# The state space branch of a hybrid block with its features on partitions

## The chip, the cores and the metric

One Trainium2 chip, of which the kernel uses one core. The metric is the device time of one execution in microseconds; less is better. The profile gives the span of one execution, from its first instruction to its last, and all rows of the trace are of that execution.

## The reference

Two layers of a decoder trunk on 512 tokens of width 1024, batch 1, all in float32. Each layer normalises `x`, multiplies it by one combined input matrix, runs three branches on pieces of the result (a Mamba-2 state space branch, latent attention, a gated delta rule), merges their projections by gates, and ends with a feed-forward part. The change touches only the state space branch:

```python
def ssd_mixer(z, xbc, dt_raw, conv_w, conv_b, dt_bias, a_log, d_skip, norm_g):
    # G = 2 groups, E = 8 heads a group, P = 64 features a head, N = 128 states
    xbc = silu(causal_dwconv(xbc, conv_w) + conv_b)
    xs, bm, cm = split(xbc, ...)
    dt = softplus(dt_raw + dt_bias); a = -exp(a_log)
    y = ssd_chunked(xs * dt[..., None], dt * a, bm, cm)
    y = y + d_skip[:, :, None] * xs
    y = y.reshape(S, SSD_INNER) * silu(z)
    y = rmsnorm(y.reshape(S, G, SSD_INNER // G), norm_g)

def ssd_chunked(X, dA, Bm, Cm):              # chunks of 128 tokens, 4 of them
    A_cum = cumsum(A)                        # within a chunk
    L = exp(where(tril, A_cum[l] - A_cum[s], -inf))
    y_diag = einsum('bcgls,bgecls,bcsgep->bclgep', Cc @ Bc.T, L, X)
    states = einsum('bclgn,bgecl,bclgep->bcgepn', Bc, exp(A_cum[-1] - A_cum), X)
    # h_prev: states carried from chunk to chunk, times exp(A_cum[-1])
    y_off = einsum('bclgn,bcgepn,bgecl->bclgep', Cc, h_prev, exp(A_cum))
    return y_diag + y_off
```

## The kernel before

Tokens are 4 tiles of 128 (`T` = 4), features 8 tiles of 128 (`KD` = 8). The normalised input lies with features on partitions, as a pair `xh`, `xl` of a rounded part and its rest. Every dense product is three TensorE matmuls of 512 moving columns (`mm3`, L181 to L183): high by high, high by low, low by high. Weights come in pieces of 512 KB over SP's DMA queue (`weights_raw`, L160, two buffers); ScalarE casts each half to its rounded part (L153), VectorE forms the rest (L154), with four buffers of each. `dense_F` leaves the result with features on partitions (the weights are stationary), two PSUM banks at a time where its piece has 256 columns; `dense_T` leaves it with tokens on partitions (the activations are stationary), four banks, one for each tile of tokens. Both take the same number of matmuls for the same weights. The PSUM banks are four for dense products (`acc`), three for small ones (`sm`) and one apart (`yt`, from `y_bank`).

A plain float32 product (operands not split, as in all small products of the state space branch) shows as two records of TensorE for each instruction, two passes.

`step_sizes`, run once a layer during the attention, computes the step sizes, the running sums of the decays and their exponentials with tokens on partitions (`dtq`, `cum`, `dec`). It writes the running sums to DRAM (`d_c`) with heads on rows, from where `seg_exp` broadcasts four heads' rows to all partitions (L455) and forms the decay matrix exp(-relu(cum[s] - cum[l])) of each head on ScalarE (L457, L458), into the tile `eE`, which has the source token s on partitions.

`ssd_group(g)` handles 8 heads. It projects and convolves B and C (`bt`, `ctl`, features on partitions), turns B to tokens on partitions (L700), projects and convolves the 512 inputs in four tiles (`xf`), and turns each by four transposes on TensorE (L708) which ScalarE copies to `xs`, tokens on partitions (L709). The gate `z` is projected by `dense_T` through `silu_T`, tokens on partitions. Then come four chunks, each with

- C times B of the chunk, masked (`cb`, L721, L723), times the decay matrices (L725);
- the inputs times the step sizes (`xd`, L727) and eight products, one for each head, with the 128 x 128 decay matrix stationary and the head's 64 inputs moving (L730);
- the skip term and the sum (L732, L733);
- from the second chunk on, C of the chunk times the carried state in one product of 512 columns (L736), scaled by the decay (L738) and added (L739);
- in all but the last, the new state (L742 to L750);
- the gate (L752) and the sum of squares over the group's 512 features, which lie on the free axis, by ScalarE's accumulator (L754).

After the chunks the row scale is formed (`rsq`, L264 and L265), the tokens' rows are scaled by it (L758), four times four transposes bring features to partitions (L763, bank `yt`), and `split_gain` (L260, L261) applies the norm's gain, a scalar for each partition there, and splits into `yh`, `yl`, the input of the branch's output projection much later.

The order of the work: `ssd_group(0)`, `gdn_decays`, half of the attention's output projection, `ssd_group(1)`, the other half, the delta-rule branch. The instructions of each engine are put in one order ahead of time by a scheduler that goes by the order of the program, by priorities and by its own estimates, so dense products of the following projection run between the chunks' small ones. On the chip each engine takes its list in that order, and so does SP with the DMAs. The big tiles of all branches share a ring of four buffers named `tok`.

## Time and profile before

| what | value |
|---|---|
| device time, median of 3 runs | 2338.18 us (2336.49 to 2344.52) |
| the profiled execution: its span | 2334.6 us |
| what lies around the span, against the median of the runs | 3.6 us |
| mean granted TensorE clock | 0.996 |
| TensorE matmul busy | 2294.8 us, 98% of the span |
| TensorE weight load busy | 1891.3 us, 81% |
| VectorE busy | 1582.1 us, 68% |
| ScalarE busy | 1159.8 us, 50% |
| DMA moved | 240.38 MB, 103 GB/s on average |

How to read it: the profile lists no device time of the profiled execution apart from its span, so a difference is worked out on the span, and the median of the runs lies 3.6 us above that. Matmuls are pipelined and their ends are modelled: the time of one is read from the start of one record to the start of the next. An engine's idle time counts only where TensorE waits for it.

### The profile page before, as it was taken

How to read it: one execution, taken by the hardware profiler on the slowest of the kernel's cores; microseconds unless marked ns; L12 is line 12 of the kernel's file. 1: busy time of each engine (PE TensorE's matmuls, PEld its weight loads, DVE VectorE, ACT ScalarE, POOL GpSimd, SP SyncE). 2: the span in 40 equal slices, each digit the busy share in tenths (PEclk: the TensorE clock that was granted, in tenths of full speed). 3: DMA queues.
4: the chain of work that ended last, by engine and by line, in shares of the span. 5: the costliest groups of instructions: out<-in, count | busy, mean ns of one | idle time of the engine just before them, and what ended most of it. 6: DMA issues, size and time to landing. Idle time of an engine off the chain costs nothing.

```text
span 2334.6 us, 32156 instructions
## 1 busy us (share of the span) xinstructions
PE 2294.8 (98%) x11926; PEld 1891.3 (81%) x11926; DVE 1582.1 (68%) x3100; ACT 1159.8 (50%) x2403; POOL 58.6 (3%) x74
## 2 busy tenths in 40 slices
PE   8999999999999999999999999999999999999998
PEld 7788787878887888888888887888788878888886
DVE  6776656875675458668767765667756645677668
ACT  6656644333443345545656557443334434545545
POOL 0000000000000000000010000000000000000000
PEclk9999999999999999999999999999999999999999
DMA  4323533352222443243132235334422224333231
GB/s 136 87 63 92 169 101 109 109 154 73 86 69 72 140 150 108 73 127 108 44 101 81 82 91 170 101 105 139 118 82 86 68 77 158 126 118 100 91 109 46
DMA packets 208221, 240.38 MB, mean 103 GB/s; under 512 B 33920, under 2 KB 155456, under 8 KB 208064
## 3 DMA queue, kind: packets, MB, share of 16 engines
q1 hardware_dynamic: 204544, 233.07, 32.7%
q10 hardware_dynamic: 3520, 5.25, 0.9%
q8 instruction: 94, 1.54, 0.3%
q14 instruction: 63, 0.52, 0.1%
HBM read 221.41 MB, written 11.63 MB: 100 GB/s over the span
## 4 chain that ended last, share of the span: by engine, by line
PE 86%; DVE 7%; DMA 3%; ACT 2%; POOL 1%; issue 1%; ACTq 0%; SPq 0%; DVEq 0%; POOLq 0%
PE acc L181 22%; PE acc L182 22%; PE acc L183 22%; PE sm L183 2%; PE sm L182 2%; PE sm L181 2%; DVE wlo L154 1%; PE sm L730 1%; DMA eE<-d_c 1%; DVE tok L846 1%; DMA mix<-mix 1%; PE sm L633 1%; DVE gQ L845 1%; PE yt L182 1%; PE sm L1003 1%
## 5 line engine op out<-in xcount | busy, mean ns | idle before, releaser
L154 DVE TENSOR_TENSOR wlo<-wraw,whi 128x512 fp32r<-128x512 f32 x552 | 378.3, 689 | 429.2 <-ACT whi L153 412.4
L153 ACT CAST whi<-wraw 128x512 fp32r<-128x512 f32 x552 | 341.4, 621 | 598.0 <-PE acc L182 371.0
L183 PE MATMUL acc<-xh,wlo 128*128 128x512 f32 (+1 forms) x1184 | 460.9, 390 | 0.0
L181 PE MATMUL acc<-xh,whi 128*128 128x512 f32 (+1 forms) x1184 | 460.7, 390 | 0.0
L182 PE MATMUL acc<-xl,whi 128*128 128x512 f32 (+1 forms) x1184 | 460.0, 389 | 0.0
L183 PEld LDWEIGHTS acc<-xh,wlo 128*128 128x128 f32 x1184 | 223.6, 189 | 41.9
L182 PEld LDWEIGHTS acc<-xl,whi 128*128 128x128 f32 x1184 | 223.5, 189 | 42.0 <-DVE xl L261 0.4
L181 PEld LDWEIGHTS acc<-xh,whi 128*128 128x128 f32 x1184 | 223.2, 189 | 41.7 <-ACT xh L260 0.4
L181 PE MATMUL acc<-yh,whi 128*128 128x512 f32 x384 | 151.9, 399 | 0.0
L182 PE MATMUL acc<-yl,whi 128*128 128x512 f32 x384 | 151.4, 394 | 0.0
L183 PE MATMUL acc<-yh,wlo 128*128 128x512 f32 x384 | 151.3, 394 | 0.0
L183 PE MATMUL acc<-whi,xl 128*128 128x512 f32 (+1 forms) x384 | 144.0, 375 | 0.0
L182 PE MATMUL acc<-wlo,xh 128*128 128x512 f32 (+1 forms) x384 | 143.9, 375 | 0.0
L181 PE MATMUL acc<-whi,xh 128*128 128x512 f32 (+1 forms) x384 | 142.6, 374 | 0.0
L674 DVE SCALAR_TENSOR_TENSOR ckl<-acc,pc,ckl 128x511 f32<-128x511 f32 (+2 forms) x168 | 120.4, 744 | 16.9 <-ACT ckl L670 8.3
L153 ACT CAST whi<-wr 128x512 fp32r<-128x512 f32 x128 | 79.5, 621 | 68.2 <-PE acc L183 32.7
L183 PE MATMUL acc<-whi,yl 128*128 128x512 f32 x256 | 99.7, 389 | 0.0
L181 PE MATMUL acc<-whi,yh 128*128 128x512 f32 x256 | 99.7, 389 | 0.0
L182 PE MATMUL acc<-wlo,yh 128*128 128x512 f32 x256 | 99.6, 389 | 0.0
L154 DVE TENSOR_TENSOR wlo<-wr,whi 128x512 fp32r<-128x512 f32 x128 | 85.8, 686 | 12.5 <-ACT whi L153 11.7
L181 PEld LDWEIGHTS acc<-yh,whi 128*128 128x128 f32 x384 | 71.7, 188 | 16.8 <-ACT yh L260 1.7
L182 PEld LDWEIGHTS acc<-yl,whi 128*128 128x128 f32 x384 | 72.2, 188 | 15.3 <-issue 1.0
(411 smaller groups left out, 4545.3 us busy)
## 6 DMA issues: line engine op xcount, KB each, us to landing
wraw<-in_w_in_dram SPq DMA_DIRECT2D x148, 512.0 KB, 3.6
wraw<-in_w_up_dram SPq DMA_DIRECT2D x64, 512.0 KB, 3.6
wr<-in_w_down_dram SPq DMA_DIRECT2D x32, 1024.0 KB, 5.0
eE<-d_c SPq DMA_DIRECT2D x48, 256.0 KB, 4.0
wraw<-in_w_mla_out_dram SPq DMA_DIRECT2D x16, 512.0 KB, 3.4
eE<-d_e SPq DMA_DIRECT2D x32, 256.0 KB, 3.0
wraw<-in_w_ssd_out_dram SPq DMA_DIRECT2D x16, 512.0 KB, 3.4
wraw<-in_w_gdn_out_dram SPq DMA_DIRECT2D x16, 512.0 KB, 3.3
```

Of the source, the lines that this page charges most:

```text
L153: act.copy(hi, raw)
L154: dve.tensor_tensor(lo, raw, f32(hi), ALU.subtract)
L181: pe.matmul(o, ah, bh, start=start, stop=False, skip_group_check=more)
L182: pe.matmul(o, ah, bl, start=False, stop=False, skip_group_check=more)
L183: pe.matmul(o, al, bh, start=False, stop=stop, skip_group_check=more)
L633: pe.transpose(ps[:, n : n + P], pn[t][:, kb * P : (kb + 1) * P], ident)
L674: dve.scalar_tensor_tensor(acc[:, d:], ps[:, : S - d], taps_[3 - d], acc[:, d:], ALU.mult, ALU.add)
L730: pe.matmul(py[:, h * 64 : (h + 1) * 64], e2[h // 4][:, h % 4, :], xd[:, h * 64 : (h + 1) * 64], start=True, stop=True)
L845: dve.tensor_tensor(pd, bc_last(nb[:, m, m + 1 :], m + 1), bc_mid(xb[:, m, : m + 1], 31 - m), ALU.mult)
L846: dve.tensor_tensor(xb[:, m + 1 :, : m + 1], xb[:, m + 1 :, : m + 1], pd, ALU.add)
L1003: pe.matmul(po[:, h * P : (h + 1) * P], pt_[:, h, :], vn[:, h * P : (h + 1) * P], start=True, stop=True)
```

## The change

The branch keeps its features on partitions to the end. The four convolved input tiles stay in `xf`, which now has a big buffer of its own; the transposed inputs are multiplied by the step sizes on the way out of PSUM (`xd`), and `xf` is then scaled in place by the skip factor, a column of parameters now. The gate is projected by `dense_F`, in two pieces of two tiles. In a chunk a head's 64 inputs are stationary, its decay matrix moves, and the two heads of a feature tile write the lower and the upper 64 partitions of one bank. The product with the carried state has four stationary pieces of 128 state columns and C moving; its decay, which now varies along the free axis, comes as a broadcast from a second DRAM copy of the exponentials (`d_p`, written in `step_sizes`), two DMAs a chunk. The sum of squares runs over partitions: a square on ScalarE, two adds on VectorE over the four feature tiles, and a product with a column of ones into the `yt` bank. The row scale goes to DRAM (`d_r`) and comes back as a broadcast over partitions; a product on VectorE with gain and row scale and `split_act` (L256, L257) take the place of the scaling, the transposes and `split_gain`. The ring `tok` has five buffers in place of four.

```diff
--- before.py
+++ after.py
@@ -31,7 +31,7 @@
 HALVES = (slice(0, S // 2), slice(S // 2, S))
 PARAMS = ('gdn_conv_w', 'ssd_conv_w', 'ssd_conv_b', 'norm1_g', 'ssd_norm_g', 'mla_q_norm_g', 'mla_kv_norm_g',
           'gdn_norm_g', 'norm2_g')
-ROWS = ('ssd_dt_bias', 'gdn_dt_bias', 'ssd_a_log', 'gdn_a_log', 'ssd_d')
+ROWS = ('ssd_dt_bias', 'gdn_dt_bias', 'ssd_a_log', 'gdn_a_log')
 
 
 def shape_constants():
@@ -299,9 +299,9 @@
 
 
     def load_params(ly, rows=True):
-        pc = mk(sp, [P, 155], F32, "pc", 2)
+        pc = mk(sp, [P, 163], F32, "pc", 2)
         sync.dma_start(pc, a["pcols"][ly])
-        prow = mk(sp, [P, 64], F32, "prow", 2)
+        prow = mk(sp, [P, 48], F32, "prow", 2)
         if rows:
             load_rows(prow, ly)
         return pc, prow
@@ -357,7 +357,7 @@
         gconv = lambda j, c: pc[:, j * 16 + c : j * 16 + c + 1]
         sconv = lambda j, c: pc[:, 64 + j * 12 + c : 64 + j * 12 + c + 1]
         col = lambda i: pc[:, 112 + i : 113 + i]
-        sconv_b, g_n1, g_ssd, g_q, g_kv, g_gdn, g_n2 = 0, 12, 20, 28, 32, 34, 35
+        sconv_b, g_n1, g_ssd, g_q, g_kv, g_gdn, g_n2, c_d = 0, 12, 20, 28, 32, 34, 35, 43
 
 
         sw = small_weights(small_raw(ly)) if ly else small_weights(raws0[0], False)
@@ -394,7 +394,8 @@
         dve.tensor_copy(sv, ps.rearrange("p (t n) -> p t n", t=T)[:, :, 64:96])
 
         cum = mk(sp, [P, T, 24], F32, "cum")
-        d_c = mk(dr, [T, 24 * P], F32, "d_c", 2)
+        d_c, d_p = (mk(dr, [T, 24 * P], F32, n, 2) for n in ("d_c", "d_p"))
+        d_r = mk(dr, [2, S], F32, "d_r", 2)
 
         def step_sizes():
 
@@ -433,6 +434,9 @@
             rows = mk(ml, [96, P], F32, "crow")
             act.copy(rows, pc_[:96, :P])
             sync.dma_start(d_c.rearrange("t (n l) -> (t n) l", l=P), rows)
+            prows = mk(ml, [96, P], F32, "crowe")
+            act.activation(prows, pc_[:96, :P], AF.Exp)
+            sync.dma_start(d_p.rearrange("t (n l) -> (t n) l", l=P), prows)
             dec = mk(sp, [P, 3, T, 24], F32, "dec")
             act.activation(dec.rearrange("p i t n -> p (i t n)"), ps[:, :288], AF.Exp)
             ndec = mk(sp, [P, T, 8], F32, "ndec")
@@ -442,8 +446,8 @@
             dve.tensor_scalar(beta, beta, 0.5, 0.5, ALU.mult, ALU.add)
             dtq = mk(sp, [P, T, 16], F32, "dtq")
             dve.tensor_scalar(dtq, spl[:, :, 0:16], 0.25, None, ALU.mult)
-            dsk = mk(sp, [P, 16], F32, "dsk")
-            dve.tensor_scalar(dsk, prow[:, 48:64], 0.25, None, ALU.mult)
+            dsk = mk(sp, [P, 8], F32, "dsk")
+            dve.tensor_scalar(dsk, pc[:, 112 + c_d : 120 + c_d], 0.25, None, ALU.mult)
             tap("spl", spl)
             tap("dec", dec)
             tap("beta", beta)
@@ -684,8 +688,7 @@
 
         def ssd_group(g, yh, yl):
             h0 = 8 * g
-            xs = mk(br, [P, T, 512], F32, "tok", 4)
-            z = mk(br, [P, T, 512], F32, "tok", 4)
+            xf, xd, z = (mk(br, [P, T, 512], F32, "tok", 5) for _ in range(3))
             bt, ctl = (mk(br, [P, S], F32, "ft", 6) if g else mk(lp, [P, S], F32, f"ckh{i}") for i in range(2))
             btok = mk(br, [P, T, P], F32, "kt", 2)
 
@@ -701,16 +704,22 @@
             act.activation(btok.rearrange("p t n -> p (t n)"), ps, AF.Copy, scale=0.25)
             for cp in range(2):
                 for j, pj in enumerate(dense_F(weights(w_in, O_XBC + 512 * g + 256 * cp, 256, D), tiles(256), D, xh, xl)):
-                    xf = mk(br, [P, S], F32, "ft4", 2)
-                    conv(pj, 4 * g + 2 * cp + j, xf)
+                    c = 2 * cp + j
+                    conv(pj, 4 * g + c, xf[:, c, :])
                     ps = sm_bank()
                     for t in range(T):
-                        pe.transpose(ps[:, t * P : (t + 1) * P], xf[:, t * P : (t + 1) * P], ident)
-                    act.copy(xs[:, :, (2 * cp + j) * P : (2 * cp + j + 1) * P], ps.rearrange("p (t n) -> p t n", t=T))
-            silu_T(br, O_SZ + 512 * g, z)
+                        pe.transpose(ps[:, t * P : (t + 1) * P], xf[:, c, t * P : (t + 1) * P], ident)
+                    th = lambda x: x.rearrange("p t (h n) -> p t h n", h=2)
+                    dve.tensor_tensor(th(xd[:, :, c * P : (c + 1) * P]), th(ps.rearrange("p (t n) -> p t n", t=T)),
+                                      bc_last(dtq[:, :, h0 + 2 * c : h0 + 2 * c + 2], 64), ALU.mult)
+                    act.activation(xf[:, c, :], xf[:, c, :], AF.Copy, scale=dsk[:, 4 * g + c : 4 * g + c + 1])
+            for cp in range(2):
+                for j, pj in enumerate(dense_F(weights(w_in, O_SZ + 512 * g + 256 * cp, 256, D), tiles(256), D, xh, xl)):
+                    silu2(z[:, 2 * cp + j, :], pj)
 
             hv8 = lambda x: x.rearrange("p (h n) -> p h n", h=8)
-            ss = mk(sp, [P, T], F32, "sss")
+            c4 = lambda x: x.rearrange("p (c l) -> p c l", c=4)
+            pss = y_bank()
             st = None
             for t in range(T):
                 tok = slice(t * P, (t + 1) * P)
@@ -723,23 +732,25 @@
                 dve.scalar_tensor_tensor(cb, ps[:, :P], 0.25, incl, ALU.mult, ALU.mult)
                 for e in e2:
                     dve.tensor_tensor(e, e, bc_mid(cb, 4), ALU.mult)
-                xd = mk(br, [P, 512], F32, "wk0")
-                dve.tensor_tensor(hv8(xd), hv8(xs[:, t, :]), bc_last(dtq[:, t, h0 : h0 + 8], 64), ALU.mult)
                 py = sm_bank()
-                for h in range(8):
-                    pe.matmul(py[:, h * 64 : (h + 1) * 64], e2[h // 4][:, h % 4, :], xd[:, h * 64 : (h + 1) * 64], start=True, stop=True)
-                y = mk(br, [P, 512], F32, "wk1")
-                dve.tensor_tensor(hv8(y), hv8(xs[:, t, :]), bc_last(dsk[:, h0 : h0 + 8], 64), ALU.mult)
-                dve.tensor_tensor(y, y, py, ALU.add)
+                for c in range(4):
+                    for i in range(2):
+                        h = 2 * c + i
+                        pe.matmul(py[64 * i : 64 * i + 64, c * P : (c + 1) * P], xd[:, t, h * 64 : (h + 1) * 64], e2[h // 4][:, h % 4, :], start=True, stop=True)
+                y = xf[:, :, tok]
+                dve.tensor_tensor(y, y, c4(py), ALU.add)
                 if t > 0:
+                    eb = mk(br, [P, 4, P], F32, f"wk{t % 2}")
+                    for i in range(2):
+                        sync.dma_start(eb[64 * i : 64 * i + 64], d_p.rearrange("t (n l) -> t n l", l=P)[t, h0 + i : h0 + 8 : 2].partition_broadcast(64))
                     po = sm_bank()
-                    pe.matmul(po, ctl[:, tok], st, start=True, stop=True)
-                    y2 = mk(br, [P, 512], F32, "wk2")
-                    dve.tensor_tensor(hv8(y2), hv8(po), bc_last(dec[:, 0, t, h0 : h0 + 8], 64), ALU.mult)
-                    dve.tensor_tensor(y, y, y2, ALU.add)
+                    for c in range(4):
+                        pe.matmul(po[:, c * P : (c + 1) * P], st[:, c * P : (c + 1) * P], ctl[:, tok], start=True, stop=True)
+                    dve.tensor_tensor(eb, c4(po), eb, ALU.mult)
+                    dve.tensor_tensor(y, y, eb, ALU.add)
                 if t < T - 1:
                     xe = mk(br, [P, 512], F32, "wk3")
-                    dve.tensor_tensor(hv8(xe), hv8(xd), bc_last(dec[:, 1, t, h0 : h0 + 8], 64), ALU.mult)
+                    dve.tensor_tensor(hv8(xe), hv8(xd[:, t, :]), bc_last(dec[:, 1, t, h0 : h0 + 8], 64), ALU.mult)
                     pst = sm_bank()
                     pe.matmul(pst, btok[:, t, :], xe, start=True, stop=True)
                     sn = mk(br, [P, 512], F32, "st", 2)
@@ -749,19 +760,22 @@
                         dve.tensor_tensor(hv8(sn), hv8(st), bc_last(dec[:, 2, t, h0 : h0 + 8], 64), ALU.mult)
                         dve.tensor_tensor(sn, sn, pst, ALU.add)
                     st = sn
-                dve.tensor_tensor(z[:, t, :], z[:, t, :], y, ALU.mult)
-                jk = mk(br, [P, 512], F32, "wk2")
-                act.activation(jk, z[:, t, :], AF.Square, accum_out=ss[:, t : t + 1])
+                zt = z[:, :, tok]
+                dve.tensor_tensor(zt, zt, y, ALU.mult)
+                sq = mk(br, [P, 4, P], F32, "wk2")
+                act.activation(sq, zt, AF.Square)
+                dve.tensor_tensor(sq[:, 0:2], sq[:, 0:2], sq[:, 2:4], ALU.add)
+                dve.tensor_tensor(sq[:, 0], sq[:, 0], sq[:, 1], ALU.add)
+                pe.matmul(pss[:, t : t + 1], sq[:, 0], ones[:, 0:1], start=True, stop=True)
             rs = mk(sp, [P, T], F32, "srs")
-            rsq(rs, ss, 1.0 / 512, EPS)
-            for t in range(T):
-                dve.tensor_scalar(z[:, t, :], z[:, t, :], rs[:, t : t + 1], None, ALU.mult)
+            rsq(rs, pss[:, :T], 1.0 / 512, EPS)
+            sync.dma_start(d_r[g].rearrange("(t p) -> p t", p=P), rs)
+            rb = mk(br, [P, S], F32, "wk0")
+            sync.dma_start(rb, d_r[g].partition_broadcast(P))
             for c in range(4):
                 k = 4 * g + c
-                ps = y_bank()
-                for t in range(T):
-                    pe.transpose(ps[:, t * P : (t + 1) * P], z[:, t, c * P : (c + 1) * P], ident)
-                split_gain(yh[k], yl[k], ps, col(g_ssd + k))
+                dve.scalar_tensor_tensor(z[:, c, :], z[:, c, :], col(g_ssd + k), rb, ALU.mult, ALU.mult)
+                split_act(yh[k], yl[k], z[:, c, :])
                 tap(f"yssd{k}", f32(yh[k]))
 
 
@@ -1264,7 +1278,8 @@
     v = {n: np.asarray(x) for n, x in inputs.items()}
     res = {n: np.ascontiguousarray(v[n]) for n in _INS}
     depth = v["w_in"].shape[0]
-    cols = np.concatenate([v[n].reshape(depth, -1, P) for n in PARAMS], axis=1)
+    cols = np.concatenate([v[n].reshape(depth, -1, P) for n in PARAMS]
+                          + [np.repeat(v["ssd_d"], 64, axis=1).reshape(depth, -1, P)], axis=1)
     res["pcols"] = np.ascontiguousarray(cols.transpose(0, 2, 1))
     res["prows"] = np.concatenate([v[n] for n in ROWS], axis=1)
     w = np.concatenate([v["w_in"][:, :, c : c + n] for c, n in ((O_KR, 64), (O_DT, 16), (O_GA, 8), (O_GB, 8))], axis=2)

...
```

Left out are four places in the delta-rule branch where a tile of the ring `tok` is asked for with five buffers in place of four, and a wider constant tile.

12 lines of the change are left out of this document (6 added, 6 removed).

## The prediction

> **What bounds the kernel now.** I read the page's engine table and the chain first, to learn which engine sets the end; then the groups by shape, to see whether the weight preparation has slack; then the busy time of the four stretches in which the chunk loop of the state space branch runs; and last the timeline of TensorE there.
>
> ```profile
> PE 2294.8 (98%) x11926; PEld 1891.3 (81%) x11926; DVE 1582.1 (68%) x3100; ACT 1159.8 (50%) x2403; POOL 58.6 (3%) x74
> PE 86%; DVE 7%; DMA 3%; ACT 2%; POOL 1%; issue 1%; ACTq 0%; SPq 0%; DVEq 0%; POOLq 0%
> ...
> L153 ACT CAST whi<-wraw 128x512 fp32r<-128x512 f32 x552 | 341.4, 621 | 598.0 <-PE acc L182 371.0
> ```
>
> TensorE is busy 98% of the span and holds 86% of the chain. ScalarE's cast of the weights, the head of the weight pipeline, idles 598 us in all, of which 371 us until a dense matmul frees a buffer: the weights stand ready and TensorE is late, not the other way round. So time is gained or lost here where TensorE's own stream gets shorter or longer, or where it has to wait. An operation on VectorE or ScalarE costs only what it makes TensorE wait.
>
> ```profile
> core 0: us, PE busy (x) PEld busy (x) DVE busy (x) ACT busy (x) POOL busy (x), PEclk, DMA share, GB/s
> 236.10:276.10 40.00, 37.91 (x192) 29.39 (x191) 31.94 (x57) 26.71 (x71) 1.01 (x1) 1.00 0.50 145
> 348.00:390.00 42.00, 40.85 (x206) 32.52 (x204) 31.46 (x54) 19.42 (x45) 0.93 (x1) 1.00 0.39 113
> 1396.00:1436.00 40.00, 38.98 (x197) 30.25 (x196) 32.37 (x57) 27.71 (x72) 1.01 (x1) 1.00 0.45 147
> 1512.00:1554.00 42.00, 41.84 (x210) 33.35 (x209) 33.54 (x59) 18.53 (x45) 1.01 (x1) 1.00 0.37 112
> ```
>
> These are the four chunk loops (two groups in each of two layers). The dense products of the output projection run between the chunks, so TensorE is idle only 2.1 + 1.2 + 1.0 + 0.2 = 4.4 us in the 164 us, at the full granted clock (1.00). VectorE is busy 129 of the 164: it has room, but not much.
>
> ```profile
> 245.22 0.39 PE L183 MATMUL acc<-xh,wlo 128*128 128x512 f32 x1
> 245.45 1.91 PE L730 MATMUL sm<-wk,eE 128*128 128x64 f32 x16
> 247.19 1.08 PE L736 MATMUL sm<-st,ckh 128*128 128x512 f32 x2
> 248.10 1.02 PE L744 MATMUL sm<-wk,kt 128*128 128x512 f32 x2
> ```
>
> From start to start (ends are modelled): a dense matmul takes 0.23 us (245.22 to 245.45). The eight head products of L730 are 16 records, two passes for each plain float32 product, in 1.74 us, 0.109 each. The product with the state (L736) is two passes in 0.91 us, that is 0.89 ns for each of 512 moving columns.
>
> ```profile
> L730 PE MATMUL sm<-wk,eE 128*128 128x64 f32 x256 | 31.9, 273 | 3.2 <-DVE eE L725 3.1
> L730 PEld LDWEIGHTS sm<-wk,eE 128*128 128x128 f32 x256 | 31.2, 191 | 11.1 <-issue 6.1 <-ACT eE L458 2.6 <-DVE wlo L154 1.0
> ```
>
> A pass of 64 moving columns would need 64 x 0.89 = 57 ns; it takes 109. The load of 128 stationary columns sets its pace, and the array streams for half of the time.
>
> **The change part by part.** All prices are TensorE's, for the 16 chunks (4 chunks, 2 groups, 2 layers), unless said.
>
> *Output transposes go.* L763 is 16 blocks of four, and one of them reads:
>
> ```profile
> 404.96 0.60 PE L763 MATMUL yt<-ct,tok 128*128 128x128 f32 x4
> 405.32 0.48 PE L183 MATMUL acc<-yh,wlo 128*128 128x512 f32 x1
> 405.63 0.40 PE L181 MATMUL acc<-yh,whi 128*128 128x512 f32 x1
> ...
> PE yt L763 <- DVE tok L758: 1.2, 2, 0.6
> ```
>
> From 404.96 to 405.63 is 0.67 us, and one dense matmul of 0.23 is in it: a block costs 0.44, of which 0.08 is the hand-over (the dense matmul behind it takes 0.31). 16 x 0.44 = 7.0 us, and the waits for VectorE in front of them, 1.2 us, go too: -8.2 us. This work lies on TensorE's path and nothing hides it, so all of it counts.
>
> *Head products: 64 stationary columns, 128 moving.* Still 16 passes a chunk, each now 128 x 0.89 = 114 ns of streaming. The two heads of a pair write PSUM partitions 0 to 63 and 64 to 127, so they are two column tiles of the array. Whether two such tiles run at once is the main unknown. The trace has no tile of 128 rows by 64 columns, but the triangular inverse of the delta-rule branch has nearby ones:
>
> ```profile
> 525.79 0.22 PE L895 MATMUL sm<-wk,ft 32*32 32x32 f32 x2
> 525.81 0.21 PE L896 MATMUL sm<-ft,wk 32*32 32x32 f32 x1
> 525.85 0.20 PE L895 MATMUL sm<-wk,ft 32*32 32x32 f32 x2
> ...
> 526.93 0.50 PE L181 MATMUL acc<-xh,whi 128*128 128x512 f32 x1
> ...
> 533.58 0.39 PE L183 MATMUL acc<-yh,wlo 128*128 128x512 f32 x1
> 533.89 0.27 PE L915 MATMUL sm<-tok,tok 64*64 64x64 f32 x1
> 533.90 0.27 PE L917 MATMUL sm<-tok,kt 64*64 64x64 f32 x1
> 534.00 0.22 PE L915 MATMUL sm<-tok,tok 64*64 64x64 f32 x1
> ...
> 534.97 0.50 PE L181 MATMUL acc<-yh,whi 128*128 128x512 f32 x1
> 535.31 0.39 PE L182 MATMUL acc<-yl,whi 128*128 128x512 f32 x1
> ...
> 529.88 1.14 PE L915 MATMUL sm<-tok,tok 64*64 64x64 f32 x16
> ```
>
> At 525.79, 96 records (32 triples of L895, L895, L896) end with the dense matmul at 526.93: 1.14 us, 0.036 a triple, while one pass of 32 columns streams for 0.028. By the code one L895 and the L896 of a triple use the same 32 rows and different columns. So column tiles over the same rows overlap. The block at 533.89 gives the price: 16 pairs on two tiles, 64 columns each, lie between the dense matmuls at 533.58 and 535.31. That is 1.73 less two dense ones (0.46), so 1.27 us: 16 pairs of 0.06 and 0.33 for going into the tiles and out. The changed chunk has 8 pairs of twice the length, which is the same sum: 1.27 against 1.74, -0.47 x 16 = -7.5 us. The weight loads fit: the last row shows 16 passes on one 64-column tile with 64 new weights each, (1.14 - 0.22) / 15 = 0.061 us apart, so two loads stay within the 0.114 of a pair. The program's order puts another product between the two halves of a chunk where the second half's decay matrices come late; each such split pays the 0.33 again. I take 4 of 16: +1.3, together -6.2 us. At the upper end the tiles don't overlap: 16 x 0.111 + 0.33 = 2.11 a chunk, +0.37 x 16 + 1.3 = +7.2 us.
>
> *Product with the state.* One product of 512 columns becomes four of 128, eight passes. The delta-rule branch has such eight:
>
> ```profile
> 621.54 1.05 PE L1003 MATMUL sm<-wk,eE 128*128 128x128 f32 x8
> 622.43 1.03 PE L1008 MATMUL sm<-st,ft 128*128 128x256 f32 x4
> ```
>
> 0.89 us for eight (0.111 a pass), where the one before took 0.91. Nothing, 12 times.
>
> *Row sums by TensorE.* The sum of squares over features now runs across partitions: two adds on VectorE, then a product with a column of ones, in each chunk. The query norm of the delta-rule branch does the same:
>
> ```profile
> 565.09 0.95 PE L935 MATMUL sm<-ct,ft 128*128 128x1 f32 x8
> 565.90 0.53 PE L944 MATMUL sm<-ct,ft 128*128 128x128 f32 x3
> ```
>
> 0.101 us a pass. Two passes and a hand-over of 0.08 make 0.28, x 16 = +4.5 us (3.2 where it stands beside another small product).
>
> *VectorE and ScalarE.* From each chunk goes the skip product and the step-size product; the latter moves to the convolution stage, straight out of PSUM, where ScalarE's copy goes and ScalarE's skip scaling comes instead. The two adds come.
>
> ```profile
> L732 DVE TENSOR_TENSOR wk<-tok,dsk 128x512 f32<-128x512 f32 x16 | 10.9, 684 | 0.0
> ...
> L758 DVE TENSOR_SCALAR tok<-tok,srs x16: 478/482/489, 273.5 to 1549.4; 128x512 f32<-128x512 f32 x16
> ...
> L723 DVE SCALAR_TENSOR_TENSOR gk<-sm,ct x16: 279/284/285, 236.8 to 1537.4; 128x128 f32<-128x128 f32 x16
> ```
>
> Between 0.284 (128 columns) and 0.684 (512) the adds of 256 and 128 columns come to an estimated 0.42 + 0.28 = 0.70, which replaces the 0.684 of L732; the chunk gets the 0.684 of the step-size product back. At a group's end four products of 0.69 replace four of 0.48, 3.3 us more VectorE in the whole kernel. The gate's dense product keeps its 96 matmuls a group and its 0.23. I cost all this at nothing, because VectorE has 35 us free in the four stretches and the casts run ahead of TensorE; if that cover were gone, the 3.3 us is its price. The second row copy and DMA behind the step sizes (one a layer) go with this.
>
> *DMAs.* Two broadcasts of the exponential rows in each chunk but the first (24), a write of the row scale and its broadcast back at each group's end (8), all on SP's queue, in front of weight loads and decay matrices.
>
> ```profile
> eE<-d_c SPq DMA_DIRECT2D x48, 256.0 KB, 4.0
> ...
> d_c<-crow SPq DMA_DIRECT2D x2, 48.0 KB, 1.9
> ```
>
> SP holds its queue while the write lands, an estimated 1.9 us, and VectorE may stand 4.0 us for the broadcast. Behind them wait weight loads and splits; four split buffers of twelve dense matmuls (2.7 us) each lie ahead of TensorE, 11 us in all, so I expect no wait from this.
>
> *New waits of TensorE.* It takes its queue in order, and the row sum stands behind a chain on VectorE and ScalarE. The nearest row is the wait that the head products have now:
>
> ```profile
> PE sm L730 <- DVE eE L725: 3.1, 4, 1.4
> ```
>
> 3.1 us, in 4 of 16 chunks, at most 1.4. VectorE has less in front of that product in the chunk, so I leave those 3.1 as they are and add 1.0 for the row sums (ends: -3.1, if the old waits go and none come, and +22, if all 16 wait 1.4).
>
> *Sum:* -8.2 - 6.2 + 0 + 4.5 + 0 + 1.0 = -8.9 us. The profiled execution has a span of 2334.6; the median of the runs, 2338.18, lies 3.6 above. 2334.6 - 8.9 = 2325.7 for the span, and 2329 us for the median. Its own ends, without split, with cheap row sums and without the old waits: -8.2 - 7.5 + 3.2 - 3.1 = -15.6, 2323 us; with three more microseconds of waits 2332.
>
> **The rivals.** *One: the column tiles take turns.* Both tiles use all 128 rows, and no row of this trace has that. Then -8.2 + 7.2 + 4.5 + 1.0 = +4.5 us, 2343 us. For it: only 32-row tiles with the same rows are seen. Against: they overlap. The Trainium skill ("TensorE: Matmul & The Clock Gate", Part 3, "The mechanism") says that a weight load overlaps a matmul in flight only where the row groups differ; by its P / 1.2 for P columns two loads of 64 would add an estimated 0.107 us to each pair, and by that rule the sum would come out at about this rival's. The trace speaks against it: on one tile, with the same rows, new weights come every 0.061 us while 0.057 is streaming.
>
> *Two: TensorE stands at each row sum* (the slower side). After the head products VectorE still adds them, scales and adds the state's part, multiplies by the gate, ScalarE squares, VectorE adds twice: 0.69 + 0.69 + 0.68 + 0.69 + 0.62 + 0.70 = 4.1 us, estimated from rows of such sizes. If the program's order places the product earlier than that chain ends by 1.4 us, each of the 16 costs 1.4: -9.9 + 22.4 = +12.5, 2351 us. It decides from 1.06 us a chunk on (17 us in all). For it: the same order misjudges L725 by up to 1.4. Against: only in 4 of 16 chunks, and the dense matmuls of the projection can be put in front.
>
> *Three: half of the gain is given back.* VectorE is the busiest helper here (79% in the four stretches); with splits in most chunks (+2.6) and a broadcast landing late in front of the next group's convolution (its transposes, L700, stand in TensorE's queue; 4.0 us at one group's end), -8.9 + 2.6 + 2.5 = about -4, 2334 us. For it: the order of all queues is written anew. Against: the 11 us of prepared weights.
>
> **How the numbers follow.** Forecast 0.58, rival one 0.12, two 0.12, three 0.18. A measurement of this kernel can tell about 0.3%, 7.0 us, from no change. Of the forecast 0.50 lies beyond that, 0.08 within; rival three and two thirds of rival one lie within; rival two and the rest are slower: faster 0.50, same 0.34, slower 0.16. The range 2321 to 2343 takes in the forecast's ends, rival three and rival one, and leaves rival two out.
>
> **What would show it.** No L763; the head products as 128*64 records with 128 moving columns, in pairs that start within some 10 ns of each other and about 0.115 us apart, a chunk's 16 in about 0.95 us; eight state passes in 0.9; 16 pairs of one-column products on the yt bank. The step on the tiles is wrong if the 16 records take 1.8 us, the one on waits if the list of TensorE's waits shows the row sums with more than 5 us, the one on cover if weight casts wait for DMA or splits end TensorE's idle time in the four stretches. The forecast is wrong if the median stays above 2332 or falls below 2323.

## The result and the profile after

The changed kernel takes 2345.78 us (median of 5 runs, 2345.22 to 2354.76) against 2338.18 (2336.49 to 2344.52): a ratio of 1.0041 [1.0025, 1.0056]. It is slower by 0.4%, where 2329 us and a gain were forecast, and the time lies 3 us outside the range. The profiled execution took 2345.22 us; its span is 2343.4, 8.8 above the one before.

The engine table and the chain by engine, on the page of the changed kernel:

```profile
PE 2288.4 (98%) x11966; PEld 1882.0 (80%) x11966; DVE 1583.0 (68%) x3116; ACT 1157.6 (49%) x2389; POOL 58.4 (2%) x74
PE 81%; DVE 7%; DMA 6%; ACT 3%; issue 1%; POOL 1%; SPq 0%; ACTq 0%; DVEq 0%; POOLq 0%
```

TensorE is busy 6.4 us less than before (2294.8), so the branch did get cheaper, and yet the span grew. The chain says where to look: TensorE's share fell from 86% to 81%, that of DMAs rose from 3% to 6%, and 2% of it is the write of the row scale alone. Next the waits of TensorE and of ScalarE, and VectorE's group that applies gain and row scale (in each row: total, times, longest, or busy time and idle time in front):

```profile
PE acc L183 <- DVE wlo L154: 9.6, 4, 3.0
...
PE sm L703 <- DVE ft L269: 2.6, 2, 2.1
...
PE acc L181 <- ACT whi L153: 1.1, 1, 1.1
```

```profile
ACT whi L153 <- DMA wraw<-in_w_mla_out_dram: 17.2, 2, 9.3
```

```profile
L777 DVE SCALAR_TENSOR_TENSOR tok<-tok,pc,wk 128x512 f32<-128x512 f32 x16 | 11.3, 746 | 44.0 <-DMA wk<-d_r 44.0
```

None of the three waits of TensorE was there before; together they are 13.3 us, 10.7 of it at the four group ends and 2.6 in the next group's convolution. VectorE stands 44.0 us for the broadcast of the row scale, 10.5 to 11.4 us at each group end. The list of DMAs has the row scale's write and its broadcast (KB each, median us from issue to landing):

```profile
wk<-d_r SPq DMA_DIRECT2D x4, 256.0 KB, 5.2
...
d_r<-srs SPq DMA_DIRECT2D x4, 2.0 KB, 10.0
```

The first group end can be read engine by engine. SyncE's queue, then VectorE, ScalarE and TensorE (start, duration, instruction, and in brackets the idle time in front and what ended it):

```profile
271.52 0.37 SPq L772 DMA_DIRECT2D d_r<-srs  x1
271.94 0.50 SPq L160 DMA_DIRECT2D wraw<-in_w_mla_out_dram  x1
272.69 0.33 SPq L802 DMA_DIRECT2D d_e<-eE  x1
282.24 0.33 SPq L774 DMA_DIRECT2D wk<-d_r  x1
...
286.73 0.43 SPq L160 DMA_DIRECT2D wraw<-in_w_mla_out_dram  x1
```

```profile
275.06 0.69 DVE L154 TENSOR_TENSOR wlo<-wraw,whi 128x512 fp32r<-128x512 f32 x1
287.17 1.42 DVE L777 SCALAR_TENSOR_TENSOR tok<-tok,pc,wk 128x512 f32<-128x512 f32 x2 [11.42 <-DMA wk<-d_r]
288.50 0.69 DVE L154 TENSOR_TENSOR wlo<-wraw,whi 128x512 fp32r<-128x512 f32 x1
```

```profile
285.70 0.62 ACT L153 CAST whi<-wraw 128x512 fp32r<-128x512 f32 x1 [9.29 <-DMA wraw<-in_w_mla_out_dram]
```

```profile
284.91 0.39 PE L183 MATMUL acc<-xh,wlo 128*128 128x512 f32 x1
286.38 0.50 PE L181 MATMUL acc<-yh,whi 128*128 128x512 f32 x1 [1.08 <-ACT whi L153]
286.71 0.40 PE L182 MATMUL acc<-yl,whi 128*128 128x512 f32 x1
289.24 0.79 PE L183 MATMUL acc<-yh,wlo 128*128 128x512 f32 x1 [2.13 <-DVE wlo L154]
289.83 0.63 PE L181 MATMUL acc<-yh,whi 128*128 128x512 f32 x1
290.26 0.63 PE L182 MATMUL acc<-yl,whi 128*128 128x512 f32 x1
...
292.71 0.39 PE L182 MATMUL acc<-yl,whi 128*128 128x512 f32 x1
```

Two things happen at once. The write is issued at 271.52, and the broadcast behind it only at 282.24, when the write has landed. VectorE's next instruction in its list is L777, so it stands from 275.75 to 287.17, and the next split (L154) waits behind it until 288.50. At the same time the weight load issued right behind the write lands 13.7 us after its issue (271.94 to 285.6), so ScalarE has nothing to cast for 9.29 us, and the half that this split needs is cast only from 285.70 to 286.32. TensorE uses up what was prepared and stands at 286.38 for the cast and at 289.24 for the split. Then it runs at half speed: 0.43 us from start to start (289.83 to 290.26) in place of 0.23, until about 292.5. The granted clock is the third number from the right in the rows by stretch (length, busy time and count of TensorE, its weight loads, VectorE, ScalarE and GpSimd, clock, DMA share, GB/s), first after, then before:

```profile
285.00:290.00 5.00, 1.79 (x6) 0.96 (x5) 2.83 (x5) 2.20 (x6) 0.00 (x0) 0.92 0.85 292
290.00:295.00 5.00, 5.00 (x18) 3.97 (x17) 1.80 (x3) 4.57 (x13) 0.00 (x0) 0.74 1.03 350
```

```profile
285.00:290.00 5.00, 5.00 (x24) 4.14 (x23) 1.39 (x2) 3.89 (x11) 0.00 (x0) 1.00 0.85 284
```

The same picture, a wait and then a stretch of about 3.4 us at half clock, stands at three of the four group ends; half clock costs half of its length, some 5 us for the three. The fourth, which has none, is the second group end, after the shortest of TensorE's waits (1.87 us).

The third group end is like the first. At the second and the fourth, the other group of each layer, the weights are not late. ScalarE, then VectorE at the second end:

```profile
399.49 0.62 ACT L153 CAST whi<-wraw 128x512 fp32r<-128x512 f32 x1 [2.14 <-PE acc L182]
```

```profile
409.38 0.68 DVE L154 TENSOR_TENSOR wlo<-wraw,whi 128x512 fp32r<-128x512 f32 x1
```

The half cast at 399.49 waits 9 us for its split, since VectorE stands for L777 from 398.25 to 408.71. TensorE's waits there, 1.87 and 2.57 us, come from VectorE alone.

In single profiles such stretches also come and go elsewhere (before has about 14 us of them in places that the change does not touch), so two profiles can't be compared closer than about 5 us. The medians can.

### The profile page after: what moved, and what is told of

Read it like the earlier page. It is cut to its first block, busy times and chain, and to the rows that moved or that the text cites. A ratio compares the mean times of both kernels' runs of the same rounds, so it can differ in the third digit from the quotient of the medians.

```text
span 2343.4 us, 32283 instructions
## 1 busy us (share of the span) xinstructions
PE 2288.4 (98%) x11966; PEld 1882.0 (80%) x11966; DVE 1583.0 (68%) x3116; ACT 1157.6 (49%) x2389; POOL 58.4 (2%) x74
## 4 chain that ended last, share of the span: by engine, by line
PE 81%; DVE 7%; DMA 6%; ACT 3%; issue 1%; POOL 1%; SPq 0%; ACTq 0%; DVEq 0%; POOLq 0%
PE acc L181 20%; PE acc L182 20%; PE acc L183 20%; PE sm L182 2%; PE sm L183 2%; PE sm L181 2%; DMA d_r<-srs 2%; DVE wlo L154 2%; DMA eE<-d_c 1%; PE sm L739 1%; DMA mix<-mix 1%; DVE tok L860 1%; ACT whi L153 1%; PE sm L637 1%; DVE gQ L859 1%
## 5 line engine op out<-in xcount | busy, mean ns | idle before, releaser
L154 DVE TENSOR_TENSOR wlo<-wraw,whi 128x512 fp32r<-128x512 f32 x552 | 377.8, 688 | 397.5 <-ACT whi L153 381.1
L183 PE MATMUL acc<-xh,wlo 128*128 128x512 f32 (+1 forms) x1312 | 509.7, 389 | 0.0
L182 PE MATMUL acc<-xl,whi 128*128 128x512 f32 (+1 forms) x1312 | 508.8, 388 | 0.0
L181 PE MATMUL acc<-xh,whi 128*128 128x512 f32 (+1 forms) x1312 | 508.8, 389 | 0.0
L182 PEld LDWEIGHTS acc<-xl,whi 128*128 128x128 f32 x1312 | 246.9, 188 | 46.7 <-DVE xl L261 0.4
L181 PEld LDWEIGHTS acc<-xh,whi 128*128 128x128 f32 x1312 | 246.5, 188 | 46.8 <-ACT xh L260 0.4
L183 PEld LDWEIGHTS acc<-xh,wlo 128*128 128x128 f32 x1312 | 246.9, 188 | 46.3
L183 PE MATMUL acc<-yh,wlo 128*128 128x512 f32 x384 | 152.4, 397 | 9.6 <-DVE wlo L154 9.6
L183 PE MATMUL acc<-whi,yl 128*128 128x512 f32 x256 | 99.7, 389 | 0.0
L183 PEld LDWEIGHTS acc<-yh,wlo 128*128 128x128 f32 x384 | 73.4, 191 | 26.2 <-DVE wlo L154 11.3
L154 DVE TENSOR_TENSOR wlo<-wr,whi 128x512 fp32r<-128x512 f32 x128 | 85.8, 686 | 12.5 <-ACT whi L153 11.7
L182 PE MATMUL acc<-wlo,xh 128*128 128x512 f32 (+1 forms) x256 | 93.9, 367 | 0.0
L183 PE MATMUL acc<-whi,xl 128*128 128x512 f32 (+1 forms) x256 | 93.6, 366 | 0.0
L181 PE MATMUL acc<-whi,xh 128*128 128x512 f32 (+1 forms) x256 | 93.3, 366 | 0.0
```

Of the source, the lines that this page charges most:

```text
L154: dve.tensor_tensor(lo, raw, f32(hi), ALU.subtract)
L181: pe.matmul(o, ah, bh, start=start, stop=False, skip_group_check=more)
L182: pe.matmul(o, ah, bl, start=False, stop=False, skip_group_check=more)
L183: pe.matmul(o, al, bh, start=False, stop=stop, skip_group_check=more)
```

## The experiments

The first theory puts the loss on the row scale's round trip through DRAM: VectorE stands for it (theory 1), or its write holds up the weight loads on the DMA queues (theory 1b). The rivals put it on the branch's own TensorE work, above all on column tiles that take turns (theory 2), or on the new order of the lists and the ring of five buffers (theory 3). Each kernel was timed in five rounds beside the kernel before on the same chip. The first four share one chip (before 2338.38 us), the next four another (2334.39), the last four a third call (2338.34), so ratios are compared across calls, and times only within one.

### The row scale spread by TensorE, without DRAM

```diff
-            sync.dma_start(d_r[g].rearrange("(t p) -> p t", p=P), rs)
-            rb = mk(br, [P, S], F32, "wk0")
-            sync.dma_start(rb, d_r[g].partition_broadcast(P))
+            dg = mk(br, [P, T, P], F32, "wk0")
+            rb = y_bank()
+            for t in range(T):
+                dve.tensor_scalar(dg[:, t, :], ones, rs[:, t : t + 1], None, ALU.mult)
+                pe.transpose(rb[:, t * P : (t + 1) * P], dg[:, t, :], ident)
```

> The changed kernel, but the row scale is spread over partitions without DRAM: VectorE writes each token's scale along 128 columns (four products of a block of ones, 0.28 us each) and TensorE transposes the four blocks into the yt bank (four passes, 0.11 us each). Theory 1 (VectorE stands 11 us at each of the four group ends for the write to DRAM and its broadcast, the prepared weight halves run out, TensorE waits 11.8 us in all and loses 5.1 us more at half clock after it): 2345.8 - 16.9 + 1.8 for the transposes = 2331 us, and no half-clock stretch after a group's end. Theory 2 (the new products themselves cost TensorE more than I priced, the waits are only where it shows): 2346 to 2348 us, as TensorE gets four passes more. Theory 3 (the new order of all queues and the larger ring cost it): 2343 to 2347 us.

Measured: 2331.14 us (2327.43 to 2332.87), ratio 0.9964 [0.9951, 0.9976]. The rest of the change is untouched, and it is now faster than before. VectorE's group, and the only wait that the new way brings:

```profile
L779 DVE SCALAR_TENSOR_TENSOR tok<-tok,pc,yt 128x512 f32<-128x512 f32 x16 | 11.2, 744 | 2.1 <-PE yt L776 2.1
```

```profile
PE yt L776 <- DVE wk L775: 2.5, 4, 0.8
```

TensorE's list of waits has no row for L183 and the splits any more. So the loss is in the round trip and what it sets off, not in the branch's products.

### The same round trip, its products after the next projection

```diff
-        ssd_group(0, *ys)
+        scale_out = ssd_group(0, *ys)      # returns the loop over L777 and split_act
         gdn_decays()
         out_proj(a["w_mla_out"][ly], 1, *y_mla, br, (0, 1))
+        scale_out()
...
```

The gain's column is copied by an operation that also reads the last merged tile of the projection, so that the products can't be taken earlier.

> The changed kernel with the same write and broadcast of the row scale, but VectorE's four products with it, and the splits, come after the half of the attention's output projection that follows (the gain they use is copied by an operation that reads the last merged tile of that half), some 25 us later in VectorE's list. Theory 1: the transfer is as long as before (10 us and 5 us) but nothing stands behind it, so 2345.8 - 16.9 = 2329 us. Theory 2: 2346 us. Theory 3: 2343 to 2347 us. If the transfers themselves disturbed the others on the DMA engines, it would also stay near 2346.

Measured: 2355.54 us (2353.41 to 2359.56), ratio 1.0072 [1.006, 1.0085]: slower than the changed kernel, a clear miss. VectorE no longer stands, but other waits took its place:

```profile
L781 DVE SCALAR_TENSOR_TENSOR tok<-tok,g,wk 128x512 f32<-128x512 f32 x16 | 11.3, 747 | 0.1
```

```profile
PE sm L703 <- DVE ft L269: 6.6, 2, 3.3
...
PE acc L181 <- ACT whi L153: 4.1, 5, 1.7
```

```profile
ACT whi L153 <- DMA wraw<-in_w_mla_out_dram: 23.2, 3, 8.5
```

The casts still wait 23.2 us for the weight loads behind the write, and the moved products now stand in front of the next group's convolution (L703 waits for L269). So VectorE's standing can't be the whole of it. The queue of transfers must be looked at by itself.

### A write of four rows in place of 512 single numbers

```diff
-            sync.dma_start(d_r[g].rearrange("(t p) -> p t", p=P), rs)
+            ps = sm_bank()
+            pe.transpose(ps[:T, :P], rs, ident)
+            row = mk(sp, [T, P], F32, "srw")
+            act.copy(row, ps[:T, :P])
+            sync.dma_start(d_r[g].rearrange("(t p) -> t p", p=P), row)
```

> The changed kernel, but the row scales are first turned by one small transpose, so that the write to DRAM is four rows of 512 bytes in place of 512 single numbers of 4 bytes. Theory 1 with a threshold: the write lands in about 2 us (as the 48 KB write of the running sums does, 1.9) instead of 10, VectorE stands about 4 us instead of 11, which the prepared weight halves cover, so all of the 16.9 us go: 2329 to 2331 us. Theory 1 without threshold (each microsecond of standing costs TensorE its part): 16.9 x 4 / 11 = 6 us remain, 2335 us. Theory 2: 2346 us; theory 3: 2343 to 2347 us.

Measured: 2330.81 us (2328.8 to 2334.66), ratio 0.9967 [0.9954, 0.998]. The trip still goes through DRAM on the same queue and is waited for in the same place; only the shape of the write is another.

```profile
L781 DVE SCALAR_TENSOR_TENSOR tok<-tok,pc,wk 128x512 f32<-128x512 f32 x16 | 11.1, 747 | 2.5 <-DMA wk<-d_r 2.5
```

VectorE stands 2.5 us in all in place of 44.0. The round trip as such is affordable; a long one is not.

### The kernel before with the round trip added

```diff
             rsq(rs, ss, 1.0 / 512, EPS)
+            d_r = mk(dr, [S], F32, "d_r", 4)
+            sync.dma_start(d_r.rearrange("(t p) -> p t", p=P), rs)
+            rb = mk(br, [P, S], F32, "wk0")
+            sync.dma_start(rb, d_r.partition_broadcast(P))
...
+            dve.tensor_tensor(rb, rb, rb, ALU.mult)    # behind split_gain
```

> The kernel before, with only the round trip added: the row scales are also written to DRAM as 512 numbers of 4 bytes, broadcast back over the partitions, and VectorE reads the broadcast in one product whose result nobody uses. Theory 1: VectorE stands at that product as it does in the changed kernel, so about 17 us are added: 2355 us (2349 to 2357), with TensorE waiting for weight halves at the four group ends. Theories 2 and 3: the round trip alone costs nothing, 2337 to 2340 us.

Measured: 2362.99 us (2359.54 to 2366.3), ratio 1.0102 [1.0088, 1.0116], 24.6 us above before.

```profile
PE acc L183 <- DVE wlo L154: 8.0, 4, 3.2
PE yt L767 <- DVE yl L261: 5.0, 2, 2.6
```

The same wait for the splits appears in a kernel that has nothing else of the change. The second row comes from the late weight load: ScalarE stands 10.0 us for it at the second group end, and behind that cast in its list lies the rounding with the gain (L260), on which, through L261, TensorE's next transposes wait. The inserted products are work for VectorE as well, and at the first and third group ends ScalarE's and SyncE's lists are ordered a little differently than before, so 24.6 is an upper bound for the trip in this kernel.

### The same round trip from GpSimd's queue

```diff
-            sync.dma_start(d_r[g].rearrange("(t p) -> p t", p=P), rs)
+            pool.dma_start(d_r[g].rearrange("(t p) -> p t", p=P), rs)
...
-            sync.dma_start(rb, d_r[g].partition_broadcast(P))
+            pool.dma_start(rb, d_r[g].partition_broadcast(P))
```

> The changed kernel with the same write and broadcast of the row scale, issued from GpSimd's DMA queue in place of SP's: SP no longer stands for the write, and no weight load is queued behind it on SP's ring, but VectorE still needs the broadcast before it goes on. Theory 1 (VectorE's standing is the cause): about as slow as the changed kernel, 2343 to 2347 us. Theory 1b (the cause is the weight load, which lands late behind the 512 numbers of the write and behind SP's standing; the run with the late products, where VectorE did not stand and TensorE waited all the same, points there): 2331 to 2336 us, with VectorE standing some 10 us and TensorE hardly waiting. Halfway between, if each alone empties the prepared halves.

Measured: 2348.3 us (2340.2 to 2352.28), ratio 1.0052 [1.0034, 1.0069].

```profile
PE acc L183 <- DVE wlo L154: 16.2, 4, 5.1
```

```profile
d_r<-srs POOLq DMA_DIRECT2D x4, 2.0 KB, 9.7
```

SyncE doesn't stand any more and its weight loads don't lie behind the write in one queue, but the write takes as long (9.7 us), VectorE stands as long (45.3 us in all), and the kernel is no faster than the changed one. Another queue doesn't shield the weights either: a weight load on SyncE's queue, issued at 269.50, 1.4 us ahead of the write on GpSimd's, lands after 9.7 us, and casts stand 9.6 us for such loads. So this run takes SyncE's standing out of the story, not the write.

### By TensorE, with the write left in and read by nobody

```diff
+            sync.dma_start(d_r[g].rearrange("(t p) -> p t", p=P), rs)
             dg = mk(br, [P, T, P], F32, "wk0")
             rb = y_bank()
```

> The version that spreads the row scale by TensorE (2331 us), with the write of the 512 numbers to DRAM added again on SP's queue and nobody reading it: nothing waits for it, neither SP nor VectorE; what is left is its place on the DMA ring in front of the next weight load. Theory 1: 2331 us. Theory 1b, if the ring alone does it: 2338 to 2345 us, with the weight load behind the write landing some 10 us late; if it also needs SP's standing: 2331 to 2334 us.

Measured: 2340.71 us (2335.47 to 2347.34), ratio 1.0024 [1.0013, 1.0035]; the same kernel without the write has 0.9964 and, run again below, 0.9979. So four writes of 2 KB that nobody waits for cost 0.45 to 0.6%, 10 to 14 us. The list of DMAs of this kernel at the first group end, from 266 to 276 us:

```profile
wraw<-in_w_mla_out_dram SPq DMA_DIRECT2D x1, 512.0 KB, 12.5
...
d_r<-srs SPq DMA_DIRECT2D x1, 2.0 KB, 9.2
```

The weight load issued right behind the write lands 12.5 us after its issue. Of the cost, the trace shows 5.0 us as waits that the version without the write doesn't have (1.8 for casts, 3.2 in front of the next group's convolution); it is of the fastest of the twelve executions, so the rest isn't placed.

### By TensorE, with the whole trip left in and read by nobody

```diff
+            sync.dma_start(d_r[g].rearrange("(t p) -> p t", p=P), rs)
+            rb2 = mk(br, [P, S], F32, "wk2")
+            sync.dma_start(rb2, d_r[g].partition_broadcast(P))
             dg = mk(br, [P, T, P], F32, "wk0")
```

> The same, with write and broadcast on SP's queue and nobody reading the broadcast: SP stands for the write, the later weight loads stand behind SP, VectorE stands for nothing. Theory 1: 2331 to 2333 us. Theory 1b: 2340 to 2346 us, close to the changed kernel, with TensorE waiting for ScalarE's cast and ScalarE for the weights.

Measured: 2339.24 us (2337.35 to 2346.51), ratio 1.0021 [1.0011, 1.0032]. That is the ratio of the write alone: that SyncE's queue stands until the write has landed adds nothing that can be measured.

### By TensorE, both heads of a pair on one column tile

```diff
-  pe.matmul(py[64 * i : 64 * i + 64, c * P : (c + 1) * P], xd[:, t, h * 64 : (h + 1) * 64], ...)
+  pe.matmul(py[0:64, c * P : (c + 1) * P], xd[:, t, h * 64 : (h + 1) * 64], ...)
...
-                dve.tensor_tensor(y, y, c4(py), ALU.add)
+                dve.tensor_tensor(y[:64], y[:64], c4(py)[:64], ALU.add)
```

> The version that spreads the row scale by TensorE, with the two heads of a pair on the same 64 partitions, so on one column tile; the second head's product overwrites the first's, and VectorE adds the lower 64 partitions only (the branch's diagonal part is incomplete). This takes away the overlap of two column tiles and nothing else. If the tiles overlap: a chunk's 16 passes go from 1.02 us to 16 x 0.114 + hand-over = about 1.9, + 0.85 x 16 = 14 us: 2345 us. If overlap is worth nothing (rival one of the prediction): 2331 us, no change.

Measured: 2341.89 us (2338.6 to 2344.79), ratio 1.0029 [1.0018, 1.0041], 0.5 to 0.65% or 12 to 15 us above the kernel with two tiles. The first chunk's head products here, and those of the changed kernel:

```profile
238.60 1.96 PE L739 MATMUL sm<-eE,tok 128*64 128x128 f32 x16
240.49 1.13 PE L755 MATMUL sm<-wk,kt 128*128 128x512 f32 x2
```

```profile
240.40 1.09 PE L739 MATMUL sm<-eE,tok 128*64 128x128 f32 x16
241.42 1.12 PE L755 MATMUL sm<-wk,kt 128*128 128x512 f32 x2
...
254.31 1.16 PE L748 MATMUL sm<-ckh,st 128*128 128x128 f32 x8
255.30 1.02 PE L755 MATMUL sm<-wk,kt 128*128 128x512 f32 x2
256.16 0.28 PE L769 MATMUL yt<-ct,wk 128*128 128x1 f32 x2
256.37 0.44 PE L739 MATMUL sm<-eE,tok 128*64 128x128 f32 x4
```

On one tile 16 passes take 1.89 us from start to start, on two 1.02. Summed over the whole kernel from start to start they take 33.6 us, and 20.9 in the version by TensorE with two tiles; the 12.7 us between them is what the medians show. The two column tiles run at once.

### The version by TensorE and the changed kernel, again

No line differs from the first experiment and from the changed kernel; both ran on one chip with the next two.

> The version that spreads the row scale by TensorE once more, as the reference point on the same chip for the three runs beside it. All theories: 0.9964 of the kernel before, as measured (within 0.995 to 0.998).

> The changed kernel once more, on the same chip as the three others. All theories: 1.0041 of the kernel before (1.0025 to 1.0056), so 0.6 to 0.9% above the version that spreads the scale by TensorE.

Measured: 2333.53 us (2329.88 to 2335.41), ratio 0.9979 [0.997, 0.9988], and 2345.47 us (2339.56 to 2351.95), ratio 1.0032 [1.002, 1.0044]. On one chip the round trip as the change has it costs 11.9 us more than the way by TensorE. The version by TensorE came out faster than before both times, by 0.2 and by 0.36%.

### VectorE stands, and the write is short

```diff
+            ps = sm_bank()                      # four rows, as above
...
+            pool.dma_start(d_r[g].rearrange("(t p) -> t p", p=P), row)
             rb = mk(br, [P, S], F32, "wk0")
-            sync.dma_start(rb, d_r[g].partition_broadcast(P))
+            pool.dma_start(rb, d_r[g].partition_broadcast(P))
+            for _ in range(2):
+                d_b = mk(dr, [P, S], F32, "d_b", 2)
+                pool.dma_start(d_b, rb)
+                pool.dma_start(rb, d_b)
```

> No write of single numbers: the row scales go out as four rows of 512 bytes and come back as a broadcast, and the broadcast is then copied to DRAM and back twice (256 KB each way, all on GpSimd's queue, so SP and its weight loads wait for nothing). VectorE needs the last copy. Theory 1 (VectorE's standing is enough): VectorE stands some 7 to 10 us at each group end, TensorE waits for weight halves there, 10 to 18 us more than the version by TensorE. Theory 1b (only the write of single numbers in front of the weight loads does it): within 4 us of the version by TensorE.

Measured: 2350.75 us (2347.75 to 2357.38), ratio 1.0059 [1.0043, 1.0075], 17 us above the version by TensorE.

```profile
302.26 1.42 DVE L785 SCALAR_TENSOR_TENSOR tok<-tok,pc,wk 128x512 f32<-128x512 f32 x2 [9.05 <-DMA wk<-d_b]
303.60 0.69 DVE L154 TENSOR_TENSOR wlo<-wraw,whi 128x512 fp32r<-128x512 f32 x1
```

```profile
PE acc L183 <- DVE wlo L154: 12.3, 2, 6.5
```

```profile
d_r<-srw POOLq DMA_DIRECT2D x4, 2.0 KB, 1.9
```

There is no write of single numbers here (four rows land in 1.9 us), and the kernel loses as much: VectorE stands 25.8 us in all, with splits behind it in its list, and TensorE 12.3 for those splits, not for a cast. The run isn't quite clean: the next group's first broadcast (L745) also stands in SyncE's queue, 8.6 us, with weight loads behind it, and the copies are more traffic. The cast of the half in question ended at 295.36, long before its split at 303.60, so these 12.3 us are VectorE's by the trace. They fall at the first and third group ends, where it stands 9.0 and 9.2 us; at the other two it stands 3.0 and 4.5 us, and TensorE doesn't wait. Of the rest of the 17, half clock behind those waits among it, that is only likely.

### The kernel before with the write alone

```diff
             rsq(rs, ss, 1.0 / 512, EPS)
+            d_r = mk(dr, [S], F32, "d_r", 4)
+            sync.dma_start(d_r.rearrange("(t p) -> p t", p=P), rs)
```

> The kernel before, with only the write of the row scales as 512 single numbers on SP's queue, which nobody reads or waits for. Theory 1b: the weight loads behind it land some 8 to 10 us late, 8 to 15 us more than the kernel before, as the same write cost in the version by TensorE (1.0024 of before against 0.9964, on two chips). Theory 1: no change, within 2 us.

Measured: 2357.75 us (2352.4 to 2363.12), ratio 1.0086 [1.0068, 1.0104], 19.4 us above before and more than was expected.

```profile
ACT whi L153 <- DMA wraw<-in_w_mla_out_dram: 15.8, 2, 8.2
```

```profile
PE yt L765 <- DVE yl L261: 5.3, 2, 2.9
PE acc L181 <- ACT whi L153: 4.1, 3, 2.6
```

Casts wait for weight loads, and TensorE for casts, with no broadcast and no waiting VectorE in the kernel. The row of L765 has the same origin. ScalarE at the second group end:

```profile
409.60 0.62 ACT L153 CAST whi<-wraw 128x512 fp32r<-128x512 f32 x1 [7.65 <-DMA wraw<-in_w_mla_out_dram]
...
411.62 0.69 ACT L260 ACTIVATE yh<-yt,pc 128x512 fp32r<-128x512 f32 x1
```

The rounding with the gain (L260) stands in ScalarE's list behind the cast that waits 7.65 us for its weights, and TensorE's transposes wait for what follows it (L261). A new order of the lists is not the reason: in the two traces VectorE's 3100 and ScalarE's 2403 instructions come in the same order as before, and SyncE's list differs by the four writes alone. So this is the cleanest of the runs: four writes of 2 KB that nobody reads cost 19.4 us. That they cost more here than in the version by TensorE fits the second wait, which that version doesn't have.

## Why the prediction was wrong, point by point

**The step that failed is the one on DMAs**: "SP holds its queue while the write lands, an estimated 1.9 us, and VectorE may stand 4.0 us for the broadcast", with "11 us in all, so I expect no wait from this". The estimate took 1.9 us from a write of 48 KB in 96 rows; this write has 512 pieces of 4 bytes and lands in 10.0 us. The broadcast takes 5.2. VectorE therefore stands 10.5 to 11.4 us at each group end and, with the one or two products of L777 that come first, ends its next split 11.8 to 13.4 us after it began to stand. The cover was smaller than reckoned too: from that moment TensorE had dense work for about 9.9 us at all four ends, not 11. The difference, 2.0 to 3.5 us, is TensorE's wait. At the first and third ends, moreover, the weight load behind the write comes 9 to 10 us late. The prediction named this sign itself: "weight casts wait for DMA or splits end TensorE's idle time". Both rows are in the profile after. The Trainium skill ("DMA: Bandwidth & Descriptors", "Specifications") gives 512 bytes as the smallest transfer at full rate; the runs agree, with 10.0 us for pieces of 4 bytes and 1.9 for four pieces of 512.

**What it cost.** Each half does it without the other: VectorE standing with a short write (1.0059 [1.0043, 1.0075] against 0.9979 [0.997, 0.9988]), the long write with nobody waiting (1.0024 [1.0013, 1.0035] in the version by TensorE, 1.0086 [1.0068, 1.0104] in the kernel before). They don't add up, since both empty the same store of prepared weights at the same time: at the first group end the cast could not start before 285.70, and VectorE was free for its split at 288.50. The trace of the changed kernel gives the second and fourth ends to VectorE; at the first and third both are late, and how the 11.9 us divide in all is not settled by these runs. Why this write delays another transfer's landing by about its own length is not shown either; only that it does.

**Half clock behind the wait** was in no step. Some 5 us, about as much as half of TensorE's waits, come from it.

**Transposes and their waits, -8.2**: right. No L763 record and no wait for L758 is left. Start to start the old transposes took 5.5 us, and the dense matmuls behind them 2.0 us more than others, so 7.5 where 7.0 was priced.

**Head products, -6.2**: right in mechanism and near in size. The 16 passes take 1.02 us where 0.95 was expected; start to start they sum to 20.9 us over the kernel, before to 27.9, so -7.0, of which about 1.2 come back in longer dense matmuls in front of them. Rival one is refuted by the kernel with one tile. With it falls the rule of the Trainium skill that the prediction weighed ("TensorE: Matmul & The Clock Gate", Part 3, "The mechanism"), as far as it would make two tiles on the same rows wait for each other's weights: two such tiles take 1.02 us for what one does in 1.89.

**Product with the state, "Nothing, 12 times"**: mis-sized. Eight passes take 0.99 us (254.31 to 255.30) where 0.89 was expected. Start to start the sums are 13.2 us against 9.4; about 1.6 of the 3.8 was charged to the dense matmuls behind the old product before, so +2 to +4 us are left.

**Row sums, +4.5**: right; they sum to 4.2 us. **New waits, +1.0, and rival two**: L769 isn't in the changed kernel's list of waits, so TensorE never stood for a row sum there. The old waits in front of the head products shrank from 3.1 us to 1.5.

**VectorE and ScalarE at nothing**: right for their work (the version by TensorE has even more of it on VectorE, 1587.7 us busy, and is faster than before). **Rival three** named the event, "a broadcast landing late", and the place behind it where TensorE would wait (the next group's convolution, 2.6 us after), but took 4.0 us at one group end.

**The sum.** Without the long trip the forecast was -8.9 us; the two versions without it measure -7.2 and -4.8 (by TensorE, in two calls) and -7.6 (four rows). That this is so near is partly luck. Over all small products of the branch and the dense matmuls around them, waits left out, TensorE's time went from 73.2 to 66.8 us, -6.4 where the sum without its waits has -8.7; the waits at transposes and head products fell by 2.8 us where the sum has -0.2. The two misses cancel. And each of the two versions pays for its own transposes (waits of 2.5 us in the first, 2.3 in the second, and the products). Both versions beat the kernel before and the changed one, and no version beyond them was run. The ring of five was not tried by itself; since these versions keep it, it can't be what made the changed kernel slow.

## What to carry to other kernels

Price a DMA by the number and size of its pieces, not by its bytes: look for a row of the same shape, and if the profile has none, take the bound as open. When an engine that prepares work for the bottleneck gets a wait in the middle of its list, count what lies behind the wait, and check that the store of prepared work isn't cut from the other side at the same time. A value for each row that must reach all partitions can go by a small transpose on TensorE, or be turned into a few long rows before it goes through DRAM.

## What the hardware showed that was not expected

- 2 KB written as 512 pieces of 4 bytes land in 8.8 to 10.0 us (medians of the eight kernels that have it, from SyncE's or GpSimd's queue), as four pieces of 512 bytes in 1.9.
- A weight load of 512 KB issued right behind such a write, 0.4 us later, lands 11.6 to 13.7 us after its issue (ten loads in five of the kernels); the medians of such loads over a whole kernel lie between 3.3 and 3.7. In the version by TensorE with the unread write (12.5 us) nothing waits for the write itself. With the write on GpSimd's queue, a load on SyncE's, issued 1.4 us ahead of the write, took 9.7 us.
- At three of four group ends, after waits of TensorE of 2.6 to 3.2 us, dense matmuls run 0.43 us apart in place of 0.23 for about 3.4 us; after the wait of 1.9 us at the fourth they don't. Such a stretch costs about 1.7 us on top of the wait.
- Column tiles of 128 rows by 64 columns run at once: 0.13 us for a pair of passes of 128 columns (1.02 / 8), though both use all rows and each pass brings new weights.
